# A fused two-block transformer kernel: table turns, four biases, the last values and two norms placed anew

## The chip, the cores and the metric

The kernel runs on one core of one Trainium2 chip. The metric is the device time of one execution in microseconds; before the change it is 2345.22 us, the median of three runs (2338.11 to 2349.35). The core has four compute engines that matter here: TensorE (PE in the profile; weight loads are listed as PEld), VectorE (DVE), ScalarE (ACT) and GpSimd (POOL). SyncE (SP) issues nearly all transfers between HBM and on-chip memory. Each engine takes its instructions in the order in which the program emits them.

## The reference, cut to what matters

One sequence of 1024 positions, 1024 channels, all in fp32. Two blocks follow each other:

```python
# first block
mod = silu(c) @ w_ada + b_ada                     # six rows of modulation
h = modulate(rms_norm(x, attn_norm_w), sh_a, sc_a)
proj = h @ w_in                                   # GLA q,k,v,r, low rank; attention Q,K,V of 4 heads
o_a = gla(forward) + gla(backward)                # chunked linear attention, 4 heads
o_b = diff_attention(Q, K, V, positions, rel_bias_table, lam)
#     s = q k^T * scale + bias[t5_bucket(key - query)];  a = softmax(s)[0] - lam * softmax(s)[1];  a @ v
x = x + g_a * (concat(o_a, o_b) @ w_out)
h2 = modulate(rms_norm(x, ffn_norm_w), sh_f, sc_f)
u = depthwise_conv3(h2 @ w_up)                    # 2 * 2816 channels
x = x + g_f * ((silu(gate) * val) @ w_down)
x = rms_norm(x, final_norm_w)

# second block
xl = x + sincos_2d(1024, 1024)
m0 = silu(c_2) @ ada_w_2[0] + ada_b_2[0]          # also with c_ctx_2, for the context
hl = rmsnorm(xl, norm_g[0]) * (1 + scale) + shift
hc = rmsnorm(ctx, norm_g[0]) * (1 + scale_c) + shift_c      # 256 context positions
u  = [hc @ w_in[:, :768], hl @ w_in[:, :768]]     # S5, both directions, started with the context
xl = xl + gate * even_mixer(hl, hc)               # S5 + FNet, gated
xl = xl + gate * odd_mixer(...)                   # pooling + short convolution, gated
return rmsnorm(xl, final_g)
```

The S5 part needs matrices that depend on its parameters alone (steps, lambda, b, c); the kernel computes them itself and calls them tables.

## The kernel before, in words

Every large product is done as three fp32r products (high by high, high by low, low by high). Weights come as fp32 into `raw` tiles, ScalarE rounds them to `hi`, GpSimd subtracts to `lo` (`split_part`, L187), all in a ring of 30 KB per partition (`Ring`, L85); `pump` (L163) loads and splits as far ahead as the ring has room.

The order on the engines is the order of emission, and it is set by a planner. Work beside the matmuls is written as generators, put into two streams (`bg`, `bg2`). While a product is emitted, `tick` (L146) is called once for every two of its k-steps, eight times for a tile of 1024 columns and eight k-steps. Each call takes the stream's rate from its wait, and while the wait is used up it runs the next piece up to its `yield`; the wait then grows by the yielded number or by the engine time that the piece is estimated to use, over 1.3, whichever is more (`Stream.step`, L76). `drain` (L153) emits whatever is left, at once. So a `yield 8.0` is a pause in planner's units and no instruction.

Stages that the change touches, in order:

- `phase1` (L428): 25 tiles of the projection. In its second part `ada` (L364) computes mod columns 16 to 23: one 128 x 1024 block of `w_ada` a step is loaded, and VectorE takes its dot with the silu'd condition; a block is loaded when the one before it is used. The lead (3.0, L564) is the yield behind each. Linear attention of the four GLA heads (`gla_head`, L715) runs in `bg` beside this. The two last tiles K3 and V3 are made half by half; between the halves the first head's q, k, v loads (`load_head`) and the biases of score tiles 0 and 1 (`load_bias`, into the weight ring) are issued. After the drain `scores(0)` emits the first score products, and then V3's `later` from `evac1` (L633): four transposes for each half, hi by ScalarE, lo by VectorE, and two stores to `v_d`. Its hi and lo (`ehi`, `elo`) are tiles of the pool `evp`, four buffers of the tag `ev`. Then the pools of the phase close.
- `phase2` (L846): a loop over g of 32 score tiles (4 heads x 8 query blocks). Each g loads the bias of g + 3 (for g + 3 > 1) and a piece of the next head, emits `scores(g + 3)`, and `expo(g + 2)`: VectorE adds the bias and takes the maximum of each of two score maps (`s<-ps_s,bias`), ScalarE takes the exponential.
- `feed_forward` (L1170): 22 gate and 22 value tiles (`ps_g`, evacuated with the depthwise convolution by VectorE into `u`), in six chunks that are each multiplied with `w_down` (`ps_d`). `bg2` holds the modulation of the second block and then `s5_tables` (L1912): parameters, a rotation table R (stored to `rot_d`), and then 24 turns. A turn reads a block `bc`, computes small products (`bs`, `bw`), and two matrices W of 128 x 512 (VectorE, and GpSimd for one factor X); one turn later `matrices` (L2088) does four transposing matmuls for each of two 288-column tiles (`ps_w`, in all eight), ScalarE copies them, and W is stored to `win_d`. After the last turn come the copies into `at0`, three sums and the stores to `t_d`.
- Before the last chunk's `w_down` product the streams are drained (L1288), then `residual` (L1019) multiplies the last five k-steps, half by half (512 positions each), eight tiles a half (`ps_x`), and adds squares for the norm. `side` is a generator that is run `pace[half]` steps at each yield of a tile's product from the second tile on: here `context` (L1339), the norm of the 256 context positions (26 steps: 2 to load, 8 of squares, 5 idle, the statistics matmul `ps_r` at step 16, one idle, nine of norm and split), followed by `block_norm(0)` (L1309: final norm, position table, squares, norm of the second block; with 9 idle steps before its own norm).
- `second_block` (L1376): `context_u(b)` for b = 0, 1, 2 multiplies the context (four yields each), running the first generator (context and half 0's norm) at each yield; then for b = 0 to 5 the products of half 0 (`ps_u`), with `context_u` for b > 2, run the second generator, half 1's `block_norm`. The latter has two idle yields before its statistics and six before its norm.

The lines that the steps of the prediction name are L564 (lead), L611 (`scores(0)`), L671 (`ehi`, `elo`), L959 and L982 (the loop's bias loads and frees), L1293 (the pace), L1314 and L1335 (idle yields), L1403 (`context_u`'s side) and L2105 (the tables' first load).

Of the kernel before, what the change touches and what calls it, by code (L numbers as in the profile page):

```python
# [20 lines left out]
T = 1024  # L21
# [99 lines left out]
class Builder:  # L121
# [306 lines left out]
    def phase1(self):  # L428
# [132 lines left out]
        self.bg2.append(self.lam())  # L561
        crow = self.cond_row(self.cond_d, glp, "crow")

        self.bg2.append(self.ada(I["w_ada"], 16, 24, self.vec("b_ada", 16, 24), [(crow, self.mod[:, 16:40])], evp, lead=3.0))  # L564
        pend = []

        def products(n, ps, **kw):
# [41 lines left out]

        self.sc = {}  # L610
        self.scores(0)  # L611
        pend.pop()()
        gl.close()
        self.hst[1].close()
# [18 lines left out]
    def evac1(self, what, ps, evp):  # L633

        nc, V, A, G, S, PE = self.nc, self.V, self.A, self.G, self.S, self.PE
        kind, i = what[0], what[1:]
        if what == "lr":
            self.lr = self.glp.tile([48, T], F32, name="lr")
            A.activation(out=self.lr, in_=ps[0:48], func=ACTF.Copy)
        elif kind in "qk":  # L640
            t = evp.tile([128, T], F32, tag="ev", name="ev")
            if kind == "q":
                A.activation(out=t, in_=ps, func=ACTF.Copy, scale=0.125)
            else:
                V.tensor_copy(out=t, in_=ps)
            S.dma_start(out=self.gqk_d["qk".index(kind), int(i)], in_=t)
        elif kind == "r":
            t = evp.tile([128, T], F32, tag="ev", name="ev")
            A.preload_act_table_set(SET_SILU)
            A.activation(out=t, in_=ps, func=ACTF.Silu)  # L650
            A.preload_act_table_set(SET_EXP)
            S.dma_start(out=self.gr_d[int(i)], in_=t)
        elif kind in "vV":

            end = what == "V3"
            vt = self.glp.tile([128, T], F32, tag="w2", name="vt") if end else evp.tile([128, T], F32, tag="ev", name="vt")
            A.activation(out=vt if kind == "v" else vt[:, ::-1], in_=ps, func=ACTF.Copy)

            def later():
                pts = []
                for g in range(2):
                    pt = self.pst.tile([128, 4, 128], F32, tag="t", name="ps_v")
                    for b in range(4):
                        PE.transpose(pt[:, b], vt[:, (4 * g + b) * 128:(4 * g + b + 1) * 128], self.eye)
                    pts.append(pt)
                if kind == "v":
                    vn = evp.tile([128, 8, 128], F32, tag="ev", name="ev")
                else:  # L670
                    hi = evp.tile([128, T], F32R, tag="ev", name="ehi")  # L671
                    lo = evp.tile([128, T], F32R, tag="ev", name="elo")
                for g, pt in enumerate(pts):
                    if kind == "v":
                        A.activation(out=vn[:, 4 * g:4 * g + 4], in_=pt, func=ACTF.Copy)
                    else:
                        h3, l3 = (x[:, g * 512:g * 512 + 512].rearrange("p (b d) -> p b d", b=4) for x in (hi, lo))
                        A.activation(out=h3, in_=pt, func=ACTF.Copy)
                        V.tensor_tensor(out=l3, in0=pt, in1=h3.bitcast(F32), op=ALU.subtract)
                if kind == "v":  # L680
                    S.dma_start(out=self.gv_d[int(i)].rearrange("p (b d) -> p b d", b=8), in_=vn)
                else:
                    S.dma_start(out=self.v_d[int(i), 0], in_=hi.bitcast(F32))
                    S.dma_start(out=self.v_d[int(i), 1], in_=lo.bitcast(F32))
            return later
        else:
            self.split_out(ps, 0.125 if kind == "Q" else 1.0, self.qk_d[int(i), "QK".index(kind)], evp, kind == "K")
        return None
# [157 lines left out]
    def phase2(self):  # L846
# [109 lines left out]

        part = 0
        for g in range(-3, NS + 2):
            if 1 < g + 3 < NS:  # L959
                self.load_bias(g + 3, bp.tile([128, T], F32, tag="b", name="bias"))  # L960
            if (g + 3) // 8 < 3:
                self.load_head((g + 3) // 8 + 1, (g + 3) % 8)
            if g in (2, 10, 18):
                self.n_max = len(self.seq)
                self.pump(g // 8, -1)
            if g >= 6 and g % 4 > 1 and part < 16:
                wo_part(part // 8, part % 8)
                part += 1
            if 0 <= g < NS:
                transp(g)  # L970
            if 0 <= g + 1 < NS:
                combine(g + 1)
            if 0 <= g - 2 < NS:
                values((g - 2) // 2, g % 2)
            for n in (0,):
                at_step(g, n)
            if 0 < g + 3 < NS:
                self.scores(g + 3)
            if 0 <= g + 2 < NS:
                expo(g + 2)  # L980
                bias.pop(g + 2)
                if g + 2 < 2:  # L982
                    self.ring.free(("bias", g + 2))
            if 0 <= g < NS:
                lows(g)
            for n in (4, 3, 2, 1):
                at_step(g, n)
# [182 lines left out]
    def feed_forward(self, side, ns):  # L1170
# [92 lines left out]
        for c, nk in enumerate(CHUNKS):  # L1263
# [20 lines left out]
            else:  # L1284
                while late:
# [4 lines left out]

                self.n_max = i + 16 + 3
                tmp = fc.enter_context(tc.tile_pool(name="nmp2", bufs=3, side="right", reuse_waits="tile"))
                side = self.residual(i, rhs, x, self.mod[:, 40:48], lambda half, acc: self.block_norm(half, acc, tmp), tmp, pace=(2, 1), lead=3,  # L1293
                                     side=self.context(tmp), keep=True)
                self.i = i + 16
            c0 += nk
# [12 lines left out]
    def block_norm(self, half, acc, tmp):  # L1309
# [1 line left out]
        x, V, A, G = self.x, self.V, self.A, self.G  # L1311
        o = slice(half * 512, half * 512 + 512)
        rs = tmp.tile([128, 512], F32, tag="rs", name="rs", bufs=2)
        if half:  # L1314
            yield
            yield
        self.rstd(acc, rs)
        yield
        acc2 = tmp.tile([128, 512], F32, tag="acc2", name="acc2", bufs=1)
# [12 lines left out]
                self.S.dma_start(out=self.x_d[:, k - 1:k + 1, o], in_=x[:, k - 1:k + 1, o])  # L1332
                yield

        for _ in range((9, 6)[half]):  # L1335
            yield
        yield from self.split_norm(x, half, acc2, self.s20, self.m20[:, 0:8], self.h[half], tmp)

# [37 lines left out]
    def second_block(self, side, fa, fc):  # L1376
# [16 lines left out]
        def context_u(b, side, pace=1, **kw):  # L1393
            pc = pcp.tile([128, 256], F32, tag="c", name="ps_c")
            for _ in self.gemm(self.i + b, lambda k, h: (self.hc[0][:, k], self.hc[1][:, k]), pc, halves=(0,), w=256, **kw):
                for _ in range(pace):
                    next(side, None)
            store_u(b, pc, 0, 32)


        before, side = side
        for b in range(3):
            context_u(b, before)  # L1403
        for _ in before:
            pass
        for b in range(6):
# [505 lines left out]
    def s5_tables(self):  # L1912
# [185 lines left out]
        def load_bc(j, d, e):  # L2098
            o = 16 * j + 8 * d + e
            bcs.append(p.tile([128, 4, 4, 16], F32, tag="bc", name="bc", bufs=2))  # L2100
            S.dma_start(out=bcs[-1], in_=I["s5_bc"][:, :, o:o + 4])

        bcs = []
        todo = [(j, d, e) for j in range(6) for d in range(2) for e in (0, 4)]
        load_bc(*todo.pop(0))  # L2105
        for j in range(6):
            for d, e in ((0, 0), (0, 4), (1, 0), (1, 4)):
                o = slice(16 * j + 8 * d + e, 16 * j + 8 * d + e + 4)
# [182 lines left out]
```

## Time and profile before

| what | value |
| --- | --- |
| median of three runs | 2345.22 us (2338.11 to 2349.35) |
| profiled execution | 2344.81 us |
| its span on the core | 2343.0 us |
| mean granted TensorE clock | 0.968 |
| PE busy | 2191.0 us (94%) |
| DVE, POOL, ACT busy | 1477.2, 996.4, 836.3 us |

The profile is one execution, so its own time stands beside its span: 1.81 us lie around the span. A row of a timeline has the start in us from the span's start, the duration, the engine, the line, the operation, what it writes and reads with shapes, how many it joins, and in brackets how long the engine stood idle before it and what ended that. L59 is the helper that records most operations of the engines, so rows of it are told apart by their tiles. Matmul ends are modelled, so two starts tell more than one duration.

### The profile page before, as it was taken

The page shows a single profiled execution, that of the slowest core. Times are in us where ns is not written, and L with a number is a line of the kernel's source. Part 1 is how long each engine was busy: PE and PEld are TensorE (multiplying, and loading weights), DVE is VectorE, ACT ScalarE, POOL GpSimd, SP SyncE. Part 2 cuts the span into 40 slices and gives each one's busy share as a digit, 9 for nine tenths or more (in the row PEclk, how much of TensorE's full clock was granted, in tenths as well). Part 3 has the DMA queues.
Part 4 walks back from the last instruction along what each step waited for, and adds up shares of the span by engine and source line. Part 5 has one row for each costly group of instructions (what it writes and reads, how often), then busy time and mean ns, then how long its engine had stood idle before and what let it go on. Part 6 is the DMA issues. An engine that isn't in the chain of part 4 may idle for free.

```text
span 2343.0 us, 28541 instructions
## 1 busy us (share of the span) xinstructions
PE 2191.0 (94%) x10168; PEld 1785.1 (76%) x10168; DVE 1477.2 (63%) x2349; ACT 836.3 (36%) x1371; POOL 996.4 (43%) x786
## 2 busy tenths in 40 slices
PE   6999999799999999999799999897978999999998
PEld 3778777687878888877588886676866777788886
DVE  8674666688365676678768777859895746221124
ACT  4335332588343222122123335432322444222223
POOL 7333223599433232222255645544443453322243
PEclk8999899999999999999899999998989999999999
DMA  7265556985433342621233334463533724111143
GB/s 273 94 189 175 177 177 187 286 236 168 172 104 120 110 156 101 220 64 60 83 123 95 124 102 134 138 192 133 181 139 135 231 86 149 50 45 50 50 153 117
DMA packets 188981, 326.71 MB, mean 139 GB/s; under 512 B 46834, under 2 KB 87698, under 8 KB 188580
## 3 DMA queue, kind: packets, MB, share of 16 engines
q1 hardware_dynamic: 188544, 324.67, 42.2%
q8 instruction: 80, 1.31, 0.2%
q14 instruction: 65, 0.53, 0.1%
q10 hardware_dynamic: 292, 0.20, 0.0%
HBM read 261.23 MB, written 67.46 MB: 140 GB/s over the span
## 4 chain that ended last, share of the span: by engine, by line
PE 65%; DVE 19%; POOL 4%; issue 4%; DMA 4%; ACT 3%; SPq 1%; DVEq 0%; POOLq 0%; ACTq 0%
PE ps_g L214 26%; PE ps_x L214 11%; PE ps_o L214 10%; PE ps_d L214 6%; DVE z L59 2%; DVE u L59 1%; POOL lo L59 1%; PE ps_s L842 1%; PE ps_u L214 1%; DVE q L59 1%; DVE sx L59 1%; PE ps_z L214 1%; PE ps_av L916 1%; DVE wa L59 1%; POOL s L59 1%
## 5 line engine op out<-in xcount | busy, mean ns | idle before, releaser
L59 POOL TENSOR_TENSOR lo<-raw,hi 128x512 fp32r<-128x512 f32 (+3 forms) x458 | 566.6, 1249 | 936.1 <-ACT hi L59 483.1
L59 ACT ACTIVATE hi<-raw 128x512 fp32r<-128x512 f32 (+3 forms) x462 | 245.8, 556 | 562.9 <-PE ps_o L214 166.0
L214 PE MATMUL ps_g<-h0hi,hi 128*128 128x512 f32 x568 | 228.5, 402 | 14.2 <-ACT h0hi L59 7.7
L214 PE MATMUL ps_g<-h1lo,hi 128*128 128x512 f32 x568 | 223.7, 394 | 6.0 <-DVE h1lo L59 6.0
L214 PE MATMUL ps_g<-h0lo,hi 128*128 128x512 f32 x568 | 223.8, 394 | 5.2 <-POOL h0lo L59 5.2
L214 PE MATMUL ps_g<-h1hi,hi 128*128 128x512 f32 x568 | 227.5, 401 | 0.0
L214 PE MATMUL ps_g<-h0hi,lo 128*128 128x512 f32 x568 | 223.4, 393 | 1.9 <-DVE lo L59 1.3
L214 PE MATMUL ps_g<-h1hi,lo 128*128 128x512 f32 x568 | 223.4, 393 | 0.0
L59 DVE SCALAR_TENSOR_TENSOR u<-ps_g,vecs,u 128x1023 f32<-128x1023 f32 (+3 forms) x94 | 114.1, 1214 | 105.2 <-ACT u L59 103.3
L214 PEld LDWEIGHTS ps_g<-h0hi,hi 128*128 128x128 f32 x568 | 108.0, 190 | 41.6 <-ACT h0hi L59 9.2
L214 PEld LDWEIGHTS ps_g<-h1lo,hi 128*128 128x128 f32 x568 | 108.0, 190 | 29.8 <-DVE h1lo L59 7.3
L214 PEld LDWEIGHTS ps_g<-h0lo,hi 128*128 128x128 f32 x568 | 107.9, 190 | 28.8 <-POOL h0lo L59 6.7
L214 PEld LDWEIGHTS ps_g<-h0hi,lo 128*128 128x128 f32 x568 | 107.8, 190 | 25.7 <-DVE lo L59 1.7
L214 PEld LDWEIGHTS ps_g<-h1hi,hi 128*128 128x128 f32 x568 | 107.8, 190 | 25.1 <-issue 2.5
L214 PE MATMUL ps_d<-acthi,hi 128*128 128x512 f32 x272 | 108.4, 399 | 18.6 <-DVE u L59 14.1
L214 PEld LDWEIGHTS ps_g<-h1hi,lo 128*128 128x128 f32 x568 | 108.1, 190 | 23.1
L59 DVE TENSOR_TENSOR acc<-acc,sq 128x512 f32<-128x512 f32 x69 | 75.8, 1100 | 54.5 <-ACT sq L59 53.5
L214 PE MATMUL ps_d<-actlo,hi 128*128 128x512 f32 x272 | 107.1, 394 | 0.0
L214 PE MATMUL ps_d<-acthi,lo 128*128 128x512 f32 x272 | 107.1, 394 | 0.0
L59 DVE TENSOR_TENSOR t<-ps_i,rot 64x480 f32<-64x480 f32 (+3 forms) x108 | 64.8, 600 | 35.3 <-PE ps_i L1508 29.1
L842 PE MATMUL ps_s<-k,q 128*128 128x512 f32 x256 | 68.9, 412 | 11.2 <-DVE mx L59 10.5
L59 POOL TENSOR_TENSOR s<-s,s 128x1024 f32<-128x1024 f32 x32 | 77.1, 2411 | 2.7
(405 smaller groups left out, 5332.2 us busy)
## 6 DMA issues: line engine op xcount, KB each, us to landing
adw<-in_ada_w_dram SPq DMA_DIRECT2D x48, 512.0 KB, 3.6
raw<-in_w_up_dram SPq DMA_DIRECT2D x88, 256.0 KB, 2.9
adw<-in_w_ada_dram SPq DMA_DIRECT2D x32, 512.0 KB, 5.0
bias<-bias_d SPq DMA_DIRECT2D x32, 512.0 KB, 4.3
raw<-in_w_in_dram SPq DMA_DIRECT2D x50, 256.0 KB, 4.0
raw<-in_odd_w_in_dram SPq DMA_DIRECT2D x48, 256.0 KB, 2.6
raw<-in_even_w_in_dram SPq DMA_DIRECT2D x44, 256.0 KB, 3.7
raw<-in_w_down_dram SPq DMA_DIRECT2D x72, 128.0 KB, 2.2
```

Of the source, the lines that this page charges most:

```text
L59: return f(*a, **k)
L214: self.PE.matmul(out, lhsT=a[:, k], rhs=b, start=first and n == 0, stop=last and n == 2)
L842: self.PE.matmul(ps[:, a * 512:a * 512 + 512], lhsT=q[:, m, qb * 128:qb * 128 + 128], rhs=kk[j][:, m, a * 512:a * 512 + 512], start=j == 0 ...
L916: PE.matmul(o, lhsT=a[:, kb], rhs=b[:, kb], start=kb + n == 0, stop=kb == 7 and n == 2)
```

## The change

Six edits. The dots in `ada` follow each other a little closer (2.8 for 3.0). The biases of score tiles 2 and 3 are loaded behind `scores(0)` into the weight ring, and the loop of phase 2 loads from tile 4. V3's hi and lo are written into two glp tiles, `U` and `sx`. The residual runs three side steps at a yield in half 0 instead of two. `block_norm` loses its two initial yields in half 1 and has 3 idle steps instead of 9 in half 0; `second_block` runs both generators in one chain beside the first three context products, with (1, 2, 1) steps a yield. `s5_tables` yields 8.0 behind its first load of bc.

```diff
@@ phase1
-        self.bg2.append(self.ada(I["w_ada"], 16, 24, ..., evp, lead=3.0))
+        self.bg2.append(self.ada(I["w_ada"], 16, 24, ..., evp, lead=2.8))
...
         self.scores(0)
+        for g in (2, 3):
+            self.load_bias(g, self.ring.tile(("bias", g), [128, T], F32, "bias"))
         pend.pop()()
@@ evac1
                 if kind == "v":
                     vn = evp.tile([128, 8, 128], F32, tag="ev", name="ev")
+                elif end:
+                    hi, lo = (self.glp.tile([128, 16, 128], F32, tag=t, name=n).bitcast(F32R).rearrange("p a d -> p (a d)")[:, 0:T]
+                              for t, n in (("U", "ehi"), ("sx", "elo")))
                 else:
                     hi = evp.tile([128, T], F32R, tag="ev", name="ehi")
                     lo = evp.tile([128, T], F32R, tag="ev", name="elo")
@@ phase2
-            if 1 < g + 3 < NS:
+            if 3 < g + 3 < NS:
                 self.load_bias(g + 3, bp.tile([128, T], F32, tag="b", name="bias"))
...
-                if g + 2 < 2:
+                if g + 2 < 4:
                     self.ring.free(("bias", g + 2))
@@ feed_forward
-  side = self.residual(i, rhs, x, ..., tmp, pace=(2, 1), lead=3, side=self.context(tmp), keep=True)
+  side = self.residual(i, rhs, x, ..., tmp, pace=(3, 1), lead=3, side=self.context(tmp), keep=True)
@@ block_norm
         rs = tmp.tile([128, 512], F32, tag="rs", name="rs", bufs=2)
-        if half:
-            yield
-            yield
         self.rstd(acc, rs)
...
-        for _ in range((9, 6)[half]):
+        for _ in range((3, 6)[half]):
             yield
@@ second_block
         before, side = side
+        both = chain(before, side)
         for b in range(3):
-            context_u(b, before)
+            context_u(b, both, (1, 2, 1)[b])
         for _ in before:
             pass
@@ s5_tables
         load_bc(*todo.pop(0))
+        yield 8.0
         for j in range(6):
```

## Rows read from the trace of the kernel before

**Rows 1.** The page: busy us, share of the span and instructions of each engine.
```profile
PE 2191.0 (94%) x10168; PEld 1785.1 (76%) x10168; DVE 1477.2 (63%) x2349; ACT 836.3 (36%) x1371; POOL 996.4 (43%) x786
```

**Rows 2.** Timelines of DVE and ACT, 422 to 444 us.
```profile
423.20 1.23 DVE L59 CUSTOM_DVE_ANT_0 adw<-adw,crow 128x1024 f32<-128x1024 f32 x1 [5.21 <-DMA adw<-in_w_ada_dram]
...
426.96 1.21 DVE L59 CUSTOM_DVE_ANT_0 s<-ps_s,bias 128x1024 f32<-128x1024 f32 x1
...
438.85 1.23 DVE L59 CUSTOM_DVE_ANT_0 s<-ps_s,bias 128x1024 f32<-128x1024 f32 x1 [3.70 <-DMA bias<-bias_d]
...
442.87 1.22 DVE L59 CUSTOM_DVE_ANT_0 s<-ps_s,bias 128x1024 f32<-128x1024 f32 x1
...
424.53 1.09 ACT L59 ACTIVATE ehi<-ps_v 128x512 fp32r<-128x512 f32 x2 [4.54 <-DMA qk_d<-ehi]
```

**Rows 3.** SP's timeline (issues), and the tile view of v_d at 426.0.
```profile
408.65 0.34 SPq L372 DMA_DIRECT2D adw<-in_w_ada_dram  x1
...
426.01 0.38 SPq L683 DMA_DIRECT2D v_d<-ehi  x1
...
DMA to landing us min/median/max: 3.5/3.5/3.5
```

**Rows 4.** Timeline of PE at 1161 us.
```profile
1161.12 0.77 PE L214 MATMUL ps_d<-acthi,hi 128*128 128x512 f32 x1 [14.13 <-DVE u L59]
```

**Rows 5.** Timeline of DVE, 1144 to 1162 us.
```profile
1146.98 0.96 DVE L59 TENSOR_TENSOR R<-Ra,Rb 128x768 f32<-128x768 f32 x1
1156.38 0.22 DVE L59 TENSOR_TENSOR bs<-bc,s 128x64 f32<-128x64 f32 x1 [8.44 <-DMA bc<-in_s_bc_dram]
...
1158.37 2.59 DVE L59 SCALAR_TENSOR_TENSOR u<-ps_g,vecs,u 128x1023 f32<-128x1023 f32 x2
```

**Rows 6.** Timeline of POOL, 1150 to 1162 us.
```profile
1153.84 0.99 POOL L59 COPY eb<-eye 128x128 f32<-128x128 f32 x4 [19.58 <-DMA rot_d<-R]
...
1159.54 1.13 POOL L59 TENSOR_TENSOR lo<-raw,hi 128x256 fp32r<-128x256 f32 x2
```

**Rows 7.** Timelines of DVE, POOL, PE and SP at the drain, 1404 to 1422 us.
```profile
1408.70 0.69 DVE L59 TENSOR_TENSOR actlo<-u,acthi 128x511 fp32r<-128x511 f32 x1 [0.70 <-ACT acthi L59]
1409.43 1.65 DVE L59 TENSOR_TENSOR s<-s,at 32x768 f32<-32x768 f32 x1
...
1409.16 6.59 POOL L59 TENSOR_TENSOR lo<-raw,hi 128x384 fp32r<-128x384 f32 x5 [14.82 <-ACT hi L59]
...
1404.51 0.47 PE L214 MATMUL ps_x<-acthi,hi 128*128 128x512 f32 x1 [1.91 <-DVE u L59]
...
1414.68 1.99 SPq L177 DMA_DIRECT2D raw<-in_w_down_dram  x4
1416.72 4.33 SPq L1348 DMA_DIRECT2D cx<-in_ctxT_dram  x4
```

**Rows 8.** The tables' last turn: DVE, PE, and the tile view of win_d at 1397.5.
```profile
1387.47 0.22 DVE L59 TENSOR_TENSOR bs<-bc,s 128x64 f32<-128x64 f32 x1
...
1390.68 0.69 DVE L59 TENSOR_TENSOR W<-W,X 128x512 f32<-128x512 f32 x1 [1.14 <-POOL X L59]
...
1395.95 1.14 PE L2093 MATMUL ps_w<-eb,W 128*128 128x144 f32 x8
...
DMA to landing us min/median/max: 2.1/2.1/2.1
```

**Rows 9.** Timeline of PE: the context's statistics.
```profile
1430.04 0.79 PE L399 MATMUL ps_r<-acc,ones 128*128 128x256 f32 x2 [1.53 <-DVE acc L59]
```

**Rows 10.** Timelines of DVE and PE: the norms of the two halves, 1490 to 1528 us.
```profile
1491.73 1.41 DVE L59 SCALAR_TENSOR_TENSOR nm<-x,s,rs 128x512 f32<-128x512 f32 x2 [4.72 <-ACT rs L59]
...
1503.71 1.42 DVE L59 SCALAR_TENSOR_TENSOR x<-x,vecs,rs 128x512 f32<-128x512 f32 x2 [0.86 <-ACT rs L59]
...
1517.44 9.31 DVE L59 TENSOR_TENSOR acc<-acc,sq 128x512 f32<-128x512 f32 x7
...
1526.81 1.13 PE L399 MATMUL ps_r<-acc,ones 128*128 128x512 f32 x2 [2.48 <-DVE acc L59]
```

More of the change, by code (lines that the diff above doesn't have):

```diff
@@ L562, in phase1 @@
         crow = self.cond_row(self.cond_d, glp, "crow")
-        self.bg2.append(self.ada(I["w_ada"], 16, 24, self.vec("b_ada", 16, 24), [(crow, self.mod[:, 16:40])], evp, lead=3.0))
+        self.bg2.append(self.ada(I["w_ada"], 16, 24, self.vec("b_ada", 16, 24), [(crow, self.mod[:, 16:40])], evp, lead=2.8))
         pend = []
@@ L1292, in feed_forward @@
                 tmp = fc.enter_context(tc.tile_pool(name="nmp2", bufs=3, side="right", reuse_waits="tile"))
-                side = self.residual(i, rhs, x, self.mod[:, 40:48], lambda half, acc: self.block_norm(half, acc, tmp), tmp, pace=(2, 1), lead=3,
+                side = self.residual(i, rhs, x, self.mod[:, 40:48], lambda half, acc: self.block_norm(half, acc, tmp), tmp, pace=(3, 1), lead=3,
                                      side=self.context(tmp), keep=True)
```

## The prediction

> **What bounds the kernel now.** I read the page first: TensorE is busy for 94% of the span, the other engines for 63% at most [rows 1]. A gain can therefore come only from TensorE's gaps, and all edits but one act in three places where it has them: the change from attention's values to the first scores (420 to 443 us), the first FFN tile with the S5 tables beside it (1147 to 1161), and the residual with the norms behind it (1404 to 1550). For each I read the timelines of VectorE, ScalarE and GpSimd for the wait that ends last, then SyncE's for the transfer behind it.
>
> The profiled execution took 2344.81 us: 2343.0 of span and 1.81 around it. The sum is made against 2344.8; the median of the three runs is 0.4 above, which is ignored.
>
> **Part A, the transition (lead, four biases, V3 elsewhere).** Three waits can go. VectorE waits 5.21 us for the last column block of w_ada, whose load was issued at 408.65 [rows 2, 3]. With lead 2.8 a product comes every 4.67 turns instead of 5 (2.8 or 3.0 divided by the rate 0.6), so the last of 24 products is 24 x 0.33 = 8, by whole turns 7, turns earlier, ahead of the 8 head loads. It then lies in head 3's scan, where its 1.23 us is hidden or, at worst, adds 1.2. ScalarE waits 4.54 us before V3's hi, as the evp buffer is still being stored [rows 2]; glp tiles U and sx are free by then. Both waits end at about 424, so what they free together is about 2.3 us. Bias 2 comes 3.70 us late [rows 2]; now it is loaded behind scores(0), ahead of the next head. All three together: -6.0.
>
> Against this stands a new wait. U and sx are handed on to phase 2: by the tiles' sizes and order, U lies where the first softmax has its second score tile and sx where its `ahi` lies. So the second score operation (428.17, just behind the one at 426.96 [rows 2]) must wait until the store of V3's hi has landed. That store was issued at 426.01 and landed 3.5 us later, 429.5 [rows 3]. From the w_ada block (423.2) to it five copies of 512 KB landed, 6.3/5 = 1.26 us apart. Now the two new biases are issued ahead of it, in all six copies behind the first K3 store that takes the block's place: 423.2 + 6 x 1.26 = 430.8. From that operation to the last of the fourth bias-score pair it is 442.87 - 428.17 = 14.7 us, 3.7 of it the bias wait [rows 2]. So that operation comes at 430.8 + 11.0 = 441.8 instead of 442.87: **-1.0**. If the store is as quick as alone (424.1 + 3.5 = 427.6), nothing new waits and it is -4 to -6; if the queue is slower and the moved product costs its 1.2, +3. I take -1, as the spacing is from the same queue in the same microseconds.
> By the Trainium skill, "DMA: Bandwidth & Descriptors", section "Queues, rings and completion order", each DMA engine takes the descriptors of one issuing engine's row in ring order, though data may finish out of order. That speaks against putting two biases ahead of a store that a wait hangs on; the 1.26 us spacing agrees with it. By the rule A is -1, by the lone store's row -4, and the whole sum would be 3 lower.
>
> The ring tiles of biases 2 and 3 are freed at g = 0 and 1, before the first weight load of that loop at g = 2, so they cost nothing; if that load came sooner, it would wait some 4 us for them.
>
> **Part B1, the tables' first turn.** TensorE idles 14.13 us before 1161.12 [rows 4]. VectorE is done with the rotation at 1147.94, but the table's first operation is next in its order and waits 8.44 us for bc, and the value tile's evacuation stands behind it (1158.37) [rows 5]. With `yield 8.0` the first turn comes ten turns later, so the evacuation (2.59 us) runs at 1147.96 to 1150.55. That does not free TensorE for good. GpSimd's four copies to eb, which stay in front of yield 8.0, wait 19.58 us for the rotation's store and run 1153.84 to 1154.83; the two lo halves of the next weight are behind them (two in 1.13 us) [rows 6]. So TensorE does five matmuls at 1150.7 (512 columns at 2.4 GHz are 0.21 us each, 1.1 in all), then waits for the first lo at 1154.83 + 0.57 = 1155.4. It goes on there instead of at 1161.12 with 1.1 us of work done: -5.7 - 1.1 = **-6.8**. Were the lo no obstacle, -10.5 (1161.12 - 1150.6); were the first turn then to hold up the next evacuation by its 2 us (1156.38 to 1158.37), or the clock lower, -4.
>
> **Part B2, the tables' end.** This is what the gain is paid with. The first turn comes 8 units, some 11 turns, later, and the planner has no slack behind it. Counted by its rule (wait += the larger of the yield and the engines' use over 1.3; rate per turn .8 or .68), before, the last table turn falls 5 to 10 turns ahead of `self.drain()` (turn 706), after, it falls past it. The last turn, the last two `matrices`, at0 with its copy, the t_d stores and the sums are then all emitted in the drain, ahead of the residual on every queue.
> On VectorE the evacuation chain ends at 1409.39 [rows 7]. Then comes a turn of 1391.37 - 1387.47 = 3.9 us [rows 8], with GpSimd's X products in it, behind what is left of its weight halves (five in 6.59 us, 1.3 each [rows 7]). So the last eight ps_w start at about 1413.4 and take 1.14 [rows 8]: ps_x begins at 1414.5 instead of 1404.51 [rows 7], 10.0 later; the two groups of ps_w no longer lie earlier, -2.3: **+7.7**. If the turn is emitted early enough to run between the evacuations, +0 to +4.
> The loads go the same way. SyncE issued the residual's next raw weights at 1414.68 and the context's loads at 1416.72 [rows 7]. Now the t_d store is ahead of both and waits for the sums, and these for the copy into at0, which waits for the stores of the matrices (landing 2.1 us [rows 8]) and then lands as long itself. 1414.5 + 2.1 + 2.1 + the sums' 4.7 (three, of which the row shows one with 1.65 [rows 7]) + issue and landing of what precedes puts the cx loads at about 1429.5, +12.8.
>
> **Part C, context in half 0.** Pace (3, 1) gives 36 side steps instead of 24, so the context's 26 end inside half 0, and its ps_r stands 15 matmuls (72 instead of 87 behind the first ps_x) earlier in TensorE's order. It now comes 1430.04 - 1416.72 = 13.3 us after the first cx load and 1.53 of it is TensorE's wait [rows 7, 9]: the chain loads, squares, adds sets it. I give it 11 us, since in that row steps wait for residual tiles between; so ps_r runs at 1429.5 + 11 = 1440.5, +10.5. TensorE reaches it at 1414.5 + 72 x 0.28 = 1434.6 (87 matmuls took 24 us of 1404.5 to 1428.5) and waits 6. It has 15 matmuls (4 us) fewer behind it, so it is 14.5 late. Some 1.5 of that comes back, as the lo halves that it waited for in this stretch are done by then: B2 and C together **+13**, 7.7 of it the drain. Bounds: +5 (ps_w early, loads on time) to +17 (chain of 13.3 and none back).
>
> **Part D, the norms.** With the idle steps 9 to 3, half 0's norm starts some 4 us sooner (it waited 4.72 us for rs at 1491.73) [rows 10]. Half 1's chain on VectorE takes 1526.75 - 1503.71 = 23.0 us [rows 10]. Its last statistics matmul now stands at the end of the fourth context product instead of in the middle of the fifth, 7 us sooner in TensorE's order, and it waited 2.48 us already [rows 10]; so it waits 7.5, and what TensorE would have done meanwhile comes after it. 4 sooner, 5 more wait: **+1** (-5 to +5).
>
> **Sum:** -1 - 6.8 + 13 + 1 = +6.2: 2344.8 + 6.2 = **2351.0**.
>
> **Rivals.**
> 1. *Faster: the tables' tail is hidden.* If the last turn is emitted before the last evacuation, or GpSimd and VectorE run it in their gaps, B2 and C cost nothing and the gains stand: -6.8 (to -10.5), -4 in A, -3 in D: 2344.8 - 13.8 = 2331.0. For it: VectorE and GpSimd are far from full [rows 1], and the slip is only some 6 turns past the drain. Against it: in order, ps_x stands behind ps_w, and the planner's count is arithmetic.
> 2. *Slower: in-order TensorE pays for each late load.* Place: the context's ps_r. From the moment the first cx load is issued after 1423.6 (11 us before TensorE's arrival at 1434.6) each further us is one us of TensorE. With the chain at 13.3 us and nothing back it is +17, with +5 in D, -1 in A and B1 at -4: 2344.8 + 17 = 2361.8. For it: TensorE's waits there were never under 1.5 us. Against it: it needs all sizes at their bad ends.
> 3. *It does not do what it says.* The gap at 1147 to 1161 stays as GpSimd's copies bind it, and the tail costs little: 2345.
>
> **How the numbers follow.** Forecast case 0.5, rival 1 0.2, rival 2 0.2, rival 3 0.1. About 0.5% (11.7 us) is what a measurement of this kernel can tell from no change, so same is 2333.5 to 2356.9. The forecast's own bounds are A +4/-5, B1 +3/-4, B2 and C +4/-8, D +4/-6; they are independent, so squares are added: +7.5/-12. It is 2339 to 2358.5. Rival 1 lies just below 2333.5 for most, 0.17 in all; rival 2 mostly above 2356.9, with a little of the forecast 0.22; the rest is 0.61. The range, 2332 to 2361, leaves out most of rival 1's gain end and half of rival 2.
>
> **What would show it.** B1 right: a short gap at 1147 to 1150.6, a second one that ends at about 1155 on GpSimd's lo. B2 right: sixteen ps_w in a row between the last ps_g and the first ps_x, this 10 us later than before (beside B1's shift), and the t_d store ahead of the residual's raw loads; wrong, if ps_x follows ps_g as now. C: the 256-wide ps_r in half 0 with some 6 us of wait. A: no bias wait, and the second score operation waiting for the store of v_d; wrong if it follows the first. D: the second 512-wide ps_r waiting some 7 us. The prediction is wrong as a whole if the tail's turns run beside the evacuations, as B2 is the largest term.

## The result and the profile after

The changed kernel takes 2357.71 us (median of five runs, 2354.96 to 2359.38), the kernel before 2346.15 us beside it. The ratio is 1.0054 with a 95% interval of 1.0034 to 1.0074, some 12.7 us (the two medians are 11.6 apart). Forecast were 2351.0 us, +6.2, in a range of 2332 to 2361: the direction held and the drain as its main cause, the size was half of what came. The time lies just above the 2356.9 up to which the prediction called it no change; that side had a chance of 0.22. The profiled execution took 2357.71 us with a span of 2355.9.

To see where the time went, the same product of TensorE (the n-th one into the same accumulator) is looked up in both traces; its start after less its start before says how late TensorE is at that point. Starts are counted from TensorE's first product (2.43 us into the span before, 2.26 after), so "late" is 0.17 more than the difference of two rows.

| point | start before | late after |
| --- | --- | --- |
| `ps_g` behind head 1's scan | 299.91 | -6.19 |
| `ps_g` ahead of head 3's scan | 395.05 | -0.79 |
| head 3's scan, first `ps_o` behind the wait | 403.08 | +0.36 |
| the product behind that scan | 408.79 | +5.48 |
| scores of tile 4 | 444.47 | +4.66 |
| last `ps_d` ahead of the gap | 1146.60 | +2.88 |
| first `ps_d` behind it | 1161.12 | -7.68 |
| `ps_g`, 25 us on | 1194.69 | -3.90 |
| `ps_g` at the last table turn of before | 1388.11 | -3.50 |
| first `ps_x` of the residual | 1404.51 | +8.53 |
| `ps_x` behind both statistics | 1449.74 | +12.68 |
| `ps_x`, late in half 1 | 1460.84 | +14.40 |
| behind both norms | 1601.94 | +13.84 |
| last product | 2333.18 | +13.06 |

The gain at 1161 is there (-6.8 when the later slow clock is paid). The residual costs +17.9. Three shifts in linear attention, all ahead of the first scores, were not in the sum: -6.2 in head 1's scan, +5.4 between 300 and 395, and +5.1 in head 3's scan. They belong to the lead, and a part of them to chance ("The moved dot" below). The rest moves by under 2 us.

*The transition.* TensorE at head 3's scan, and the window around it (span; PE, PEld, DVE, ACT and POOL busy; granted clock; DMA share; GB/s); VectorE's first two score operations; SyncE's issues:
```profile
403.27 1.12 PE L816 MATMUL ps_o<-qi,sx 128*128 128x64 f32 x4 [2.90 <-DVE sx L59]
...
392.00:422.00 30.00, 27.10 (x113) 23.19 (x113) 12.13 (x31) 4.46 (x6) 0.00 (x0) 0.77 0.74 197
...
429.77 1.22 DVE L59 CUSTOM_DVE_ANT_0 s<-ps_s,bias 128x1024 f32<-128x1024 f32 x1
...
435.52 1.23 DVE L59 CUSTOM_DVE_ANT_0 s<-ps_s,bias 128x1024 f32<-128x1024 f32 x1 [4.53 <-DMA v_d<-ehi]
...
427.39 1.18 SPq L362 DMA_DIRECT2D bias<-bias_d  x2
...
429.04 0.33 SPq L688 DMA_DIRECT2D v_d<-ehi  x1
```
The bias wait of [rows 2] is gone, and in its place the second score operation waits for the store of V3's hi, which is issued behind two biases: the exchange that was forecast. New is the first pair: TensorE idled 2.90 us ahead of `ps_o` (1.76 before), and the clock is 0.77 over the 30 us; the 46 products of the scan take 10.1 us, 5.35 before.

*The tables' first turn.* TensorE, VectorE, GpSimd:
```profile
1153.27 0.70 PE L214 MATMUL ps_d<-acthi,hi 128*128 128x512 f32 x1 [3.57 <-DVE u L59]
...
1158.41 0.80 PE L214 MATMUL ps_d<-acthi,lo 128*128 128x512 f32 x1 [2.74 <-POOL lo L59]
...
1150.53 2.60 DVE L59 SCALAR_TENSOR_TENSOR u<-ps_g,vecs,u 128x1023 f32<-128x1023 f32 x2
...
1156.68 1.00 POOL L59 COPY eb<-eye 128x128 f32<-128x128 f32 x4 [19.75 <-DMA rot_d<-R]
1157.63 1.99 POOL L59 TENSOR_TENSOR lo<-raw,hi 128x256 fp32r<-128x256 f32 x3
```
Against [rows 4 to 6]: the gap of 14.13 us has become 3.57, five products, and 2.74 for a lo that stands behind GpSimd's copies, as forecast.

*The drain.* VectorE, GpSimd, TensorE, the window of 1404 to 1415 and SyncE's issues:
```profile
1404.99 0.69 DVE L59 TENSOR_TENSOR actlo<-u,acthi 128x511 fp32r<-128x511 f32 x1 [0.69 <-ACT acthi L59]
1405.59 1.01 DVE L59 TENSOR_TENSOR bs<-bc,s 128x64 f32<-128x64 f32 x1
1406.53 0.76 DVE L59 TENSOR_TENSOR bx<-bc,s 128x64 f32<-128x64 f32 x1
...
1410.15 0.69 DVE L59 TENSOR_TENSOR W<-W,X 128x512 f32<-128x512 f32 x1 [1.14 <-POOL X L59]
...
1416.10 0.70 DVE L59 MEMSET at<- 32x768 f32 x1 [3.02 <-DMA win_d<-W]
...
1405.44 1.77 POOL L59 TENSOR_TENSOR lo<-raw,hi 128x384 fp32r<-128x384 f32 x2 [6.89 <-ACT hi L59]
...
1410.98 2.26 PE L2096 MATMUL ps_w<-eb,W 128*128 128x144 f32 x8 [11.96 <-DVE W L59]
...
1404.00:1415.00 11.00, 4.02 (x13) 3.68 (x14) 6.23 (x14) 4.83 (x13) 5.01 (x5) 0.50 0.16 63
...
1424.49 0.39 SPq L2171 DMA_DIRECT2D t_d<-s  x1
1424.97 2.00 SPq L177 DMA_DIRECT2D raw<-in_w_down_dram  x4
1427.07 1.32 SPq L1350 DMA_DIRECT2D cx<-in_ctxT_dram  x3
```
Where before had `ps_x` after 1.91 us [rows 7], TensorE now waits 11.96 us for the last turn's W and does the last eight ps_w at the clock of 0.50. The t_d store stands ahead of the raw weights and of the context's loads.

*The context's statistics* come behind two waits of TensorE (1.53 in [rows 9]):
```profile
1433.62 0.79 PE L214 MATMUL ps_x<-acthi,hi 128*128 128x512 f32 x1 [3.52 <-ACT hi L59]
1438.40 1.19 PE L399 MATMUL ps_r<-acc,ones 128*128 128x256 f32 x2 [1.63 <-DVE acc L59]
```

### The profile page after: what moved, and what is told of

It is laid out like the page before. It is cut to its first block, busy times and chain, and to the rows that moved or that the text cites. A ratio compares the mean times of both kernels' runs of the same rounds, so it can differ in the third digit from the quotient of the medians.

```text
span 2355.9 us, 28547 instructions
## 1 busy us (share of the span) xinstructions
PE 2195.5 (93%) x10168; PEld 1789.5 (76%) x10168; DVE 1466.9 (62%) x2349; ACT 836.2 (35%) x1371; POOL 997.0 (42%) x786
## 5 line engine op out<-in xcount | busy, mean ns | idle before, releaser
L59 DVE CUSTOM_DVE_ANT_0 s<-ps_s,bias 128x1024 f32<-128x1024 f32 x64 | 75.6, 1216 | 4.8 <-DMA v_d<-ehi 4.5
```

Of the source, the lines that this page charges most:

```text
L59: return f(*a, **k)
```

## Experiments

Ratios are to the kernel before on the same chip, with 95% intervals; 0.001 is 2.35 us. "Late" is read as in the table above.

| kernel | ratio | interval |
| --- | --- | --- |
| after | 1.0054 | 1.0034 to 1.0074 |
| after, lead 3.0 | 1.0034 | 1.0022 to 1.0047 |
| before, lead 2.8 | 1.0003 | 0.9989 to 1.0017 |
| after, no yield | 1.0022 | 1.0009 to 1.0035 |
| before, yield 8.0 | 1.0028 | 1.0015 to 1.0041 |
| after, V3 in evp | 1.0038 | 1.0025 to 1.0051 |
| after, old norms | 1.0046 | 1.0031 to 1.0062 |
| before, yield 1.5 | 0.9972 | 0.9957 to 0.9987 |
| before, yield 1.5, biases, idle 3 | 0.9971 | 0.9958 to 0.9985 |
| before, new norms | 1.0012 | 1.0000 to 1.0024 |
| before, yield 1.5, copies later | 0.9984 | 0.9970 to 0.9998 |
| after, biases behind V3's stores | 1.0043 | 1.0027 to 1.0058 |
| before, transition alone | 1.0008 | 0.9990 to 1.0025 |

### The yield of 8.0, taken out and alone

```diff
         load_bc(*todo.pop(0))
-        yield 8.0
```


> The changed kernel without yield 8.0, all else as changed. Theory (the tables' tail in the drain is the price): the idle time of 14 us before 1161 comes back (+7.5), the sixteen ps_w leave the drain and the context's loads go out some 10 us sooner (-17), so 2357.7 + 7.5 - 17 = about 2348. Rival (the new order of the norms is the price, the tail costs little): the gain at 1161 is lost and little comes back, about 2362 to 2365.

```diff
         load_bc(*todo.pop(0))
+        yield 8.0
```


> The kernel before with yield 8.0 and nothing else. Theory (the tail is the price, whatever the norms): -7.5 at 1161, +13 at the first ps_x, and less than 4 at the context's statistics, as these stand 15 matmuls later in TensorE's order than in the changed kernel: 2346 + 6 to 9 = 2352 to 2355. Rival (the tail hides behind the old order of the norms): 2338 to 2342.

Without it 1.0022, alone 1.0028: it costs 6.6 us by itself and some 7.5 of the change's 12.7. Its two ends are the same in either setting. Alone, TensorE goes from 10.63 late at 1146.60 to 2.29 late at 1194.69 (-8.3), and from 2.72 late at 1388.11 to 14.76 at the first `ps_x`: +12.04, in the changed kernel +12.03. Without it both are gone. So the tail in the drain is the price, whatever the order of the norms; the rivals of both runs fall. For the kernel without it the size was off by some 3 us (2351.3 by the ratio, 2348 expected): of the 17 us that were to come back in the residual, 4.4 stay (4.15 late at 1388.11, 8.52 at 1460.84). The new norms alone cost the same 4.4 there (below).

### A yield of 1.5

```diff
         load_bc(*todo.pop(0))
+        yield 1.5
```


> The kernel before with yield 1.5 at the place where the change has 8.0, and nothing else. Theory (the gain needs only that the first table turn falls behind the value tile's evacuation, the loss comes from the last turn falling past the drain): the first ps_d resumes as early as in the changed kernel, -6.5 to -8; the table turns come one or two turns later only, the last still ahead of the drain, ps_x follows ps_g as before: about 7 us less than the kernel before, a ratio of 0.997. Rival (the gain at 1161 is paid back wherever the turns lie, because the same work on VectorE and GpSimd is only moved): 0.999 to 1.001.

0.9972 (0.9957 to 0.9987): 6.6 us less than before, 13 less than with 8.0. TensorE's rows at the gap and at the drain, and VectorE's at the drain:
```profile
1147.09 0.62 PE L214 MATMUL ps_d<-acthi,hi 128*128 128x512 f32 x1 [3.57 <-DVE u L59]
1152.15 0.80 PE L214 MATMUL ps_d<-acthi,lo 128*128 128x512 f32 x1 [2.73 <-POOL lo L59]
...
1396.60 0.80 PE L214 MATMUL ps_x<-acthi,hi 128*128 128x512 f32 x1 [3.53 <-DVE u L59]
...
1394.35 0.70 DVE L59 MEMSET at<- 32x768 f32 x1 [2.20 <-DMA win_d<-W]
```
The gap is as short as with 8.0. No ps_w stands ahead of `ps_x`; what is left of the slip is the memset of at, which waits 2.20 us for win_d ahead of the last evacuation and costs `ps_x` 1.6 us (3.53 instead of 1.91). This version beats both kernels.

### Copies to eb behind the yield

```diff
-        for eb in ebs:
-            for g in range(2):
-                G.tensor_copy(out=eb[:, g, 16:144], in_=self.eye)
...
         load_bc(*todo.pop(0))
+        yield 1.5
+        for eb in ebs:
+            for g in range(2):
+                G.tensor_copy(out=eb[:, g, 16:144], in_=self.eye)
```


> The kernel before with yield 1.5 and with GpSimd's four copies to eb behind that yield instead of ahead of it. Theory (GpSimd in its order holds the lo halves behind the wait for the rotation's store): TensorE's second wait of 2.73 us for lo at 1152 goes; 2 to 3 us less than with yield 1.5 alone, a ratio of 0.9955 to 0.9965. Rival (the weights' raw loads behind the bc load on SyncE are late as well): TensorE waits for ScalarE's hi at nearly the same time, the ratio stays at 0.997.

0.9984, no better than yield 1.5 alone, the intervals overlap. The wait for lo is gone, another has come:
```profile
1144.24 0.76 PE L214 MATMUL ps_d<-acthi,hi 128*128 128x512 f32 x1 [4.28 <-DVE u L59]
1153.38 0.56 PE L214 MATMUL ps_d<-acthi,hi 128*128 128x512 f32 x1 [1.98 <-DVE x L59]
```
From 1146.60 to 1194.69 it gains 4.6 us, yield 1.5 alone 5.6: the theory's cause was right, its price nil, as VectorE, which had waited for bc, now has a table turn ahead of the next evacuation. The rival, a wait for ScalarE's hi in its place, did not show.

### The moved dot

```diff
-  ... evp, lead=2.8))
+  ... evp, lead=3.0))
```


> The changed kernel with the lead of the w_ada dots back at 3.0, all else as changed. Theory (the moved dot): the last dot in head 3's scan lengthened TensorE's idle time before ps_o from 1.76 to 2.90 us, and behind that the granted clock stood at 0.50 for some 10 us; without it the scan runs at the full clock, the bias wait stays away, and the time falls by 6 to 7 us, from 2357.7 to about 2351; the windows 404 to 412 show a clock of 1.00 and 54 or so matmuls. Rival (the clock wanders by itself): the half clock is not tied to the dot, the time stays at 2356 to 2359 or the half clock turns up in the same place.

```diff
-  ... evp, lead=3.0))
+  ... evp, lead=2.8))
```


> The kernel before with the lead at 2.8 and nothing else. Theory (the moved dot): idle before head 3's ps_o about 2.9 us, the granted clock at 0.50 behind it, TensorE some 6 us late at 416; the wait of 5.21 us for w_ada goes but V3's hi still waits for the evp buffer; the time rises by 5 to 6 us to about 2351.5. Rival (the dot is hidden, as the prediction costed it): 2345 to 2347, no half clock.

With lead 3.0 the changed kernel stands at 1.0034, 4.7 us less where 6 to 7 were expected, but the two intervals overlap; with 2.8 the kernel before stands at 1.0003 (-2.6 to +4.0 us). The 5 to 6 us that the second run's theory asked for did not come, although the long idle time and the half clock did; so the times do not settle what the lead costs. The traces say more. The idle time of TensorE ahead of `ps_o` and the time that a stretch of the same products takes, in all fourteen profiles, sorted by lead (us; a fall is one of the granted clock from 1.00 to 0.50):

| stretch (start before) | lead 3.0, 7 kernels | lead 2.8, 7 kernels |
| --- | --- | --- |
| head 1's scan (240 to 270) | idle 1.93 to 1.94; 23.6, but 28.5 to 30.1 in four with a fall | idle 0.97 to 0.98; 22.7, no fall |
| head 3's gates, ahead of `ps_f` (345 to 385) | idle 1.51 to 1.52; 40.1, no fall | idle 3.30 to 4.34; 43.5 to 45.9, a fall in all seven |
| head 3's scan (395 to 411) | idle 1.73 to 1.76; 15.9, but 20.8 in one with a fall (yield 1.5) | idle 2.87 to 2.90; 21.9 to 23.1 in six with a fall, 17.1 in one (without yield) |

Lead 3.0 is the kernel before, after with lead 3.0, and before with yield 8.0, 1.5, 1.5 with biases, 1.5 with copies, and new norms; lead 2.8 is the other seven. In head 3's scan the 46 products alone took 5.35 us where the clock stayed up, otherwise 8 to 10. By the means of seven the lead gives 4.0 us in the first stretch and costs 4.9 in the second and 4.8 in the third.

The loss in the second stretch is hard to see in the first two profiles, as a fall in head 1's scan had cost the kernel before as much. Its cause is a load. With lead 2.8 a dot ahead of head 3's gates waits 4.5 to 5.3 us for its block of w_ada in all seven, with 3.0 in none, and all of the head's work on VectorE stands behind it. VectorE and TensorE after, TensorE before, and the window of 364 to 372 after and before:
```profile
348.75 1.23 DVE L59 CUSTOM_DVE_ANT_0 adw<-adw,crow 128x1024 f32<-128x1024 f32 x1 [4.99 <-DMA adw<-in_w_ada_dram]
...
364.35 0.99 PE L773 MATMUL ps_f<-qi,ki 64*128 64x128 f32 x5 [3.80 <-DVE ki L59]
...
368.42 0.82 PE L768 MATMUL ps_f<-qi,ki 64*128 64x128 f32 x5 [1.52 <-DVE ki L59]
...
364.00:372.00 8.00, 7.65 (x29) 6.31 (x30) 3.47 (x5) 0.50 (x1) 6.15 (x4) 0.57 0.20 83
...
364.00:372.00 8.00, 6.48 (x37) 5.19 (x36) 8.00 (x8) 2.81 (x4) 6.30 (x4) 1.00 0.63 206
```
So the smaller lead moved every dot and not only the last, and the wait of 5.21 us for w_ada that it took away at 423 [rows 2] it put in at 349. Of what head 3's scan costs a part comes back behind it, as other waits shrink: from 395 to 445 the five kernels with lead 3.0 and the transition as before take 49.4 to 51.3, 50.2 in the mean, the kernel before with lead 2.8 takes 52.9, 2.6 more. An estimate from these rows is -4.0 + 4.9 + 2.6 = +3.5 for the lead; both timings allow it.

The idle times are certain; the clock behind them is a matter of odds, four of seven behind 1.94 us, one of seven behind 1.76, six of seven behind 2.90, all seven behind 3.30 and more, none of seven behind 1.52 or 0.98. By the Trainium skill, "TensorE: Matmul & The Clock Gate", section "HAM oscillation — how this bites in real kernels", waits for DMA of some 3 to 5 us between stretches of matmuls bring the array back to the lower clock each time. The falls behind 3.30 to 4.34 us agree, in all seven; here shorter waits were enough too, in some of the profiles.

### The transition: V3's tiles, the order of the biases, all three alone

```diff
-                elif end:
-                    hi, lo = (... for t, n in (("U", "ehi"), ("sx", "elo")))
```


> The changed kernel with V3's hi and lo back in the evp buffers, all else as changed. Theory (the tiles handed on to phase 2 make the new wait): the second score operation of VectorE follows the first at once instead of waiting 4.5 us for the store of v_d; ScalarE waits for K3's store before V3's hi again, some 2 us; the third bias is there in time. 4 to 5 us less than the changed kernel, a ratio of about 1.0035 to the kernel before. Rival (the queue of 512 KB copies sets the pace, whoever waits): the bias or the head's loads come later by as much, the time stays at 1.005.

```diff
         self.scores(0)
-        for g in (2, 3):
-            self.load_bias(...)
         pend.pop()()
+        for g in (2, 3):
+            self.load_bias(...)
```


> The changed kernel with the loads of biases 2 and 3 behind V3's two stores instead of ahead of them. Theory (the two biases ahead of the store in SyncE's queue make the new wait as long as it is): the second score operation waits some 2 to 2.5 us less for the store of v_d, but the 16 DMA engines are full from 404 to 460, so the bias then comes late by about as much; the time stays within 2 us of the changed kernel, 1.0045 to 1.0055. Rival (the store's wait is the bound and the bias has slack): 2 to 3 us less at the ninth score product and after it, 1.004.

The kernel before with lead 2.8, the biases and V3's tiles:

> The kernel before with the three edits of the transition alone: lead 2.8, biases 2 and 3 behind the first scores, V3's hi and lo in U and sx. Theory (what is freed is taken by the wait for the store of v_d, and the moved dot lengthens TensorE's idle time in head 3's scan): what the parts leave over, the changed kernel's +12.7 less +6.6 of yield 8.0 and +2.8 of the norms, is +3.3, a ratio of 1.001 to 1.0015; the second score operation waits 4 to 6 us for the store. Rival (the prediction's own step A, a store that lands 1.26 us a copy): -1, a ratio of 0.999 to 1.000.

With V3 in evp the ratio is 1.0038, 4 us less as expected, though within the intervals; the second score operation follows the first, at 429.51 behind 428.37. With the biases behind the stores it is 1.0043 (1.0027 to 1.0058), between theory and rival, and the wait for the store shrinks from 4.53 to 0.82 us:
```profile
433.41 1.23 DVE L59 CUSTOM_DVE_ANT_0 s<-ps_s,bias 128x1024 f32<-128x1024 f32 x1 [0.82 <-DMA v_d<-ehi]
...
451.66 1.23 DVE L59 CUSTOM_DVE_ANT_0 s<-ps_s,bias 128x1024 f32<-128x1024 f32 x1 [1.64 <-DMA bias<-bias_d]
```
So it is the order in SyncE's queue that makes that wait. By the Trainium skill's rule that the prediction cited ("DMA: Bandwidth & Descriptors", section "Queues, rings and completion order") each DMA engine takes the copies of one issuing engine in the order of their issue; 4.53 against 0.82 us agree. Counted from behind the scan, the kernel with the late biases is 2.9 us better off at tile 4 than the changed one, but only 1.1 at 465 us, as a later bias comes 1.64 us late. The transition alone is at 1.0008 (0.9990 to 1.0025), which leaves -1 and +3 both open; in its trace the second score operation waits 4.57 us for the store, and from behind the scan to 465 us TensorE loses 0.2.

### Three waits at once

The edits, condensed:
```diff
+        yield 1.5                       # s5_tables
...
+        for g in (2, 3): self.load_bias(...)   # behind scores(0), loop from 3 < g + 3
...
-        for _ in range((9, 6)[half]):
+        for _ in range((3, 6)[half]):
```


> The kernel before with yield 1.5, with biases 2 and 3 loaded behind the first scores as changed, and with 3 idle steps instead of 9 before half 0's norm; lead 3.0, V3 in evp, pace and chains as before. Theory (each of these three takes a wait away and hands none on): -7 at 1161, -3 in the first scores, -4 at the first ps_u, together about -14, a ratio of 0.994. Rival (the waits are only moved: the biases push the stores of V3 back in the queue, the earlier norm meets squares that are not done): the ratio of yield 1.5 alone, 0.997.

0.9971, what yield 1.5 gives alone: the theory fell, and the waits are only moved, as the rival had it, though to a later bias and not to V3's stores. VectorE's row and the windows of 436 to 452, then TensorE's at half 0's norm:
```profile
447.82 1.23 DVE L59 CUSTOM_DVE_ANT_0 s<-ps_s,bias 128x1024 f32<-128x1024 f32 x1 [4.73 <-DMA bias<-bias_d]
...
436.00:444.00 8.00, 6.85 (x34) 4.63 (x35) 6.50 (x14) 6.37 (x12) 7.59 (x7) 1.00 1.04 211
444.00:452.00 8.00, 4.29 (x20) 3.44 (x19) 3.96 (x8) 3.03 (x6) 3.17 (x3) 0.85 1.03 237
...
1485.76 2.08 PE L399 MATMUL ps_r<-acc,ones 128*128 128x512 f32 x2 [8.89 <-DVE acc L59]
```
Bias 2 is there in time and TensorE 4.15 us early at score tile 3, but bias 4 comes 4.73 us late, and at tile 5 the gain is gone. The DMA engines are full (1.03 to 1.04): loading two biases sooner makes the next ones later. And half 0's statistics, moved up, wait 8.89 us for squares that are not done.

### The norms

> The changed kernel with the residual's pace (2, 1), the idle steps and the two generators of the second block as in the kernel before; the tables, the biases and V3 as changed. Theory (TensorE meets the context's and the second half's statistics sooner in its own order and waits there): 3 to 5 us less than the changed kernel, a ratio of 1.003 to 1.004. Rival (the new order of the norms gains, as the earlier norm of half 0 suggests): 2 to 4 us more, a ratio of 1.006 to 1.007.

> The kernel before with the edits of the norms alone: pace (3, 1), no initial yields in half 1, 3 idle steps in half 0, both generators beside the first context products. Theory (TensorE meets statistics matmuls sooner than VectorE has their sums): +2 to 3 at the context's statistics, +2 in the rest of the residual, -4 at the first ps_u, +5 at half 1's second statistics, together +3 to 5, a ratio of 1.0015 to 1.002. Rival (the change of the norms only costs behind a drain that is late): -1 to +1, a ratio of 0.9995 to 1.0005.

The first is the changed kernel with `pace=(2, 1)`, `(9, 6)`, the two yields and `context_u(b, before)`; the second the kernel before with the new ones. 1.0046 against 1.0054 is within the intervals and decides nothing; alone the new norms are at 1.0012 (1.0000 to 1.0024), +2.8 us, just below the theory's 3 to 5, and the interval still touches the rival's -1 to +1. Their trace: 2.3 early at the first `ps_x`, 2.2 late at 1460.84 (+4.4), 5.8 early at the start of `ps_u` (half 0's norm comes sooner), 3.1 late at 1517.27, 1.6 late behind both norms. What the first half gains is given back at the second half's context products.

## Why the prediction was right in kind and half in size

| part | forecast | changed kernel's trace | timed alone |
| --- | --- | --- | --- |
| A, up to 444 us | -1 | +4.7 | +1.9 (-2.4 to +5.9) |
| B1 | -6.8 | -6.8 | |
| B2 (first `ps_x`) | +7.7 | +12.0 | |
| B2 and C (1388 to 1461) | +13 | +17.9 | |
| D | +1 | -0.6 | |
| all | +6.2 | +13.1 | +12.7 |

The yield alone is +6.6, the new norms alone +2.8, the transition +1.9: with 11.3 in sum they make up the 12.7 within the intervals. The trace's +4.7 in A counts from a profile of before that had lost some 6 us by a fall in head 1's scan; that trace and times agree in the sum (13.1 and 12.7) is in part luck.

**A.** The exchange itself was right. In the kernel without the yield, where the clock stayed up, the store's arrival lets the second score operation go at 430.79, where 430.8 was forecast, and TensorE moves from -0.2 behind the scan to 0.0 at 444:
```profile
430.79 1.22 DVE L59 CUSTOM_DVE_ANT_0 s<-ps_s,bias 128x1024 f32<-128x1024 f32 x1 [6.07 <-DMA v_d<-ehi]
```
The step that failed is the lead: the prediction moved the last dot alone, "hidden or, at worst, adds 1.2". That dot, 1.2 us on VectorE, is not hidden (idle 1.76 to 2.90), and in the profiled execution the scan ran at half clock behind it, 4.7 us more. The dots ahead of it moved too, which the sum did not hold: one waits 4.99 us for its load ahead of head 3's gates and costs 5.4 us, one frees 1 us in head 1's scan. That the lead brings these idle times is shown by all fourteen profiles; that it brings the falls is likely from their count, and what it costs in all is not settled by the times.

**B1.** Right in each step: evacuation at once, five products, a wait that ends on GpSimd's lo behind its copies. The first product gains 10.6; the second wait takes 2.9 of it, and the lower clock behind it, which stood in the bounds and not in the sum, another 2.1. Groups of ps_w that now come later give back 1.2. So the mechanism was foreseen, but that the net comes out at -6.8 to a tenth is luck.

**B2.** The mechanism was right: sixteen ps_w between the last `ps_g` and the first `ps_x` (eight at 1397.88, eight at 1410.98), and t_d ahead of the loads. The size was off by 4.3, since the turn was priced from one row of a quiet stretch. VectorE's evacuation ends at 1405.68 and W is there at 1410.84: 5.2 us, 3.9 by [rows 8]. The first two small products took 1.01 and 0.76 us there instead of 0.22. They lie beside two lo halves of GpSimd (1405.44 to 1407.21), the third, behind these, takes 0.22 again, and in [rows 8] GpSimd stood idle beside them; that GpSimd is the cause is likely and not shown, as no run took it away. At the clock of 0.50 `ps_x` begins 1.89 us behind the first ps_w, not 1.14. And the 2.3 us that the ps_w groups were to give back did not come: TensorE's last `ps_g` is 0.9 earlier than at 1388 (-4.39 against -3.50), but the evacuation behind it, with the turn ahead of the last in between, is not (-3.54). 1.3 + 0.75 + 2.3 make the 4.3.

**C.** Behind the first `ps_x` the forecast added 5.3, the trace 5.9. The wait of "6 us" at the context's statistics came as 3.52 for the raw weights, that the same t_d store delays, and 1.63 for the sums: 5.15. The chain of 11 us from the first cx load to ps_r measured 1438.40 - 1427.07 = 11.3, but the load came 2.4 sooner than the forecast 1429.5; the wait for the raw weights, which the sum did not hold, filled the place.

**D.** Forecast +1 (4 sooner, 5 later), came -0.6, by two terms of nearly twice the size that cancel: TensorE goes from 14.40 late to 6.5 at 1501.73 and back to 15.35 at 1517.27. So the small sum is in part luck. The second statistics of half 1 wait 1.57 us only, not 7.5; the context product ahead of them had already waited 1.71, 1.08 and 0.74 for its weights, which is 3.5 of the missing 5.9:
```profile
1523.22 0.38 PE L214 MATMUL ps_c<-hchi,lo 128*128 128x256 f32 x1 [1.71 <-POOL lo L59]
1525.75 0.58 PE L214 MATMUL ps_c<-hchi,hi 128*128 128x256 f32 x1 [1.08 <-ACT hi L59]
1527.29 0.58 PE L214 MATMUL ps_c<-hchi,lo 128*128 128x256 f32 x1 [0.74 <-POOL lo L59]
1531.37 2.08 PE L399 MATMUL ps_r<-acc,ones 128*128 128x512 f32 x2 [1.57 <-DVE acc L59]
```

**The rivals.** The hidden tail (2331) fell: the last turn's ps_w found no gap in front of `ps_x`. That every us of late loads costs a us (2361.8) came near in time, but by the drain's size, the clock and the lead rather than by the context's chain. The cancelling (2345) fell: the gap went, and the yield alone is clear of 1.

## What to carry to other kernels

A pause in a planned stream shifts all that follows: look up how much slack lies before the next drain, and take the smallest pause that moves the one blocked step (1.5 gave the whole gain, 8.0 lost it twice over). In a stretch where the DMA engines are full, an earlier load makes another later; and a tile handed on to the next phase carries its store's place in the queue along. A smaller pause between loads moves every one of them, not only the last that was in the way: look at each wait in the stretch. Price work that falls into a drain as a chain in which each engine waits for the last, and not by a row from a quiet stretch; here TensorE's clock had fallen to 0.50 by then. And compare single profiles with care: one fall of the clock in head 1's scan (some 6 us) hid a loss of 5.4.

## What was not expected of the hardware

1.14 us more on VectorE lengthened an idle time of TensorE from 1.76 to 2.90 us; behind it the granted clock was 0.50 for most of the next 8 to 10 us in six of seven profiles, against one of seven with the shorter wait. Behind 1.94 us, ahead of the same kind of scan, it fell in four of seven. What decides between profiles with the same wait stayed open.
